# Split parts for four units' gates, a bank of its own for a chain's last product, and other ranks for copies and splits

## The chip, the cores and the metric

The kernel runs on one core of a Trainium2 chip. The metric is the time of one execution in microseconds, as the device takes it; the time before is the median of three timed runs. A separate execution was profiled, and every row of a trace below is from that one.

## The reference

The program is one layer of a decoder trunk over a sequence of 2048 positions with 1024 features, in float32.

```python
h = rms_norm(x, norm1_g)
z = h @ w_in                                   # 1024 -> 3584
lru_x, lru_gate, sc_b, sc_c, sc_x = split(z)   # 1024, 1024, 512, 512, 512
lru_x = causal_dwconv(lru_x, lru_conv_w) + lru_conv_b          # 4 taps
r = sigmoid(lru_x @ wa + ba); i = sigmoid(lru_x @ wx + bx)     # 16 heads of 64
a = exp(-8 r softplus(-lam)); b = sqrt(1 - a^2) * (i * lru_x)
y_lru = scan(h = a h + b) * gelu(lru_gate)
y_sc = sc_b * causal_dwconv(sc_c * sc_x, sc_conv_w)            # 3 taps
x = x + concat(y_lru, y_sc) @ w_out
h = rms_norm(x, norm2_g)
gate, up = split(causal_dwconv(h @ w_up, ffn_conv_w))          # 1024 -> 6144
x = x + (gelu(gate) * up) @ w_down
return rms_norm(x, final_g)
```

## The kernel before, in words

Features lie on the 128 partitions and positions along the free dimension. The sequence is worked on in two halves of 1024 positions (T); a matmul covers a block of 512 (NB). The order of the stages is: in-projection and out-projection of the first half (0 to 332 and 332 to 449 us of the span), the same of the second half (449 to 743 and 743 to 862), then up- and down-projection of the first half (to 1322 and 1551) and of the second (to 2008 and the end).

**Split products.** A float32 product is made of three products in TensorE's one-pass float32 format (fp32r): each operand is split into a high part (a copy on ACT that rounds, L239) and a low part (a subtraction on DVE, L240), and the products hi·hi, hi·lo and lo·hi are added in PSUM (`product_step`, L291, matmuls at L295). The weights of every output block are loaded by SP into a page "wr" and split into "wh" and "wl". One small product was not split: the gates.

**The first half's in-projection** (`in_phase`, L491) begins with the eight blocks of x. Each is loaded, scaled and split into xh and xl (L463, L464), and its products with two (for two blocks three) weight blocks are started at once. Its square (ACT, L309) is added to ss_a (DVE, L310); when all eight are in, the sum is itself split (rh_a, rl_a), multiplied by a matrix of 1/1024 on PE (ms_a, L327), and gives 1/rms, with which every later result is scaled as it leaves PSUM. After that the units follow in the order L0 L1 S0 S1 L2 L3 L4 L5 L6 L7 S2 S3: eight recurrent units (L, 128 channels, two heads of 64 on two halves of the partitions) and four short-convolution units (S). In a recurrent unit PE makes the gate branch's product of this unit and the product of the next one (96 matmuls), then this unit's gates (`lru_gates`, L376, matmuls at L380): for each block of 512 and each half of the partitions one float32 matmul with a 64x128 weight block from "gw", out into four PSUM banks zr and zi. Their moving operand is cv, the unit's convolution (ACT L354, then three DVE steps L356). ACT then takes the sigmoids of the gates (eight of 64x512, L391), and exp, tanh, square and square root in turn (L396 to L400), DVE the scan, and the product with the gelu of the gate branch (L407) is y.

**What is written off.** Results y and combinations of them (yc, yd, made by DVE at L562 to L569) are stored by POOL to the DRAM buffers y_d some steps later (`defer`, `tick`, L236). POOL also adds weight blocks to each other in DRAM by accumulating transfers (so_d, L418). Small temporary tiles (squares, rh, rl, yc, yd, gw) share a pool "tmp" of seven pages of 128x1024: a new tile there waits for the last reader of the page it gets, a store included.

**The second half's in-projection** (`in_blocks`, L907; class `InPair`, L854) multiplies pairs of output blocks by Strassen's scheme with seven products over four 512-wide operands: W11, W12, W22, S1 to S4. A product is 12 matmuls (four K steps, three split products, L689), and three banks serve it: x collects W11, S2, S3 and W22 one after the other, and after each of them ACT copies the running sum out (`copy`, L700), so that the next product in the bank has to wait for the copy; a holds W12; c holds S1 and S4. DVE adds the banks to the copies (`add`, L704). Each turn of the loop works on one pair (`cur`) and finishes the one before it (`prev`): W11 and W12 of cur, W22 of prev, the gates of the last finished recurrent unit, S2 of cur, S4 of prev, and S1 and S3 of cur. In the trace the tiles of the pairs are called xlin, prin, sbin (a pair's first block) and soin (its second), and the banks zxin, zain, zcin.

**What sets the order.** PE, SP and POOL run in the order in which the program is written. On DVE and ACT a scheduler orders the instructions by priority: `tc.high_priority(offset=n)` ranks a block of them n steps ahead of its place in the program. The copies and additions of the pairs, the sigmoids and the results that leave PSUM all have HP = 120; weight splits of the first half have HW = 90; the splits of the second in-projection, the squares and the convolutions of the first half have none.

## Time and profile before

| | us |
|---|---|
| median of three timed runs | 2259.07 (2258.54 to 2259.25) |
| the profiled execution | 2254.52 |
| its span | 2252.5 |
| PE busy in the span | 2223.2 (99%) |
| DVE busy | 1780.7 (79%) |
| ACT busy | 1216.2 (54%) |
| POOL busy | 175.7 (8%) |
| first half's in-projection: 34 to 332 of the span | PE busy 298.0 of 298 |
| second half's, with the first part of its out-projection: 449 to 780 | PE busy 318.9, DVE 240.3, ACT 243.0 of 331 |

PE's granted clock is 0.998 over the span. An engine's row in a timeline begins with the start and the duration in microseconds, then the engine, the source line, the operation, the tiles out<-in and their shape; in square brackets stands how long the engine was idle before the instruction and what ended the wait. A matmul's own duration overlaps the next one's, so the distance of two starts tells its cost. In a table of waits the three numbers are the sum, how often, and the longest.

### The profile page before, as it was taken

The page shows a single profiled execution, that of the slowest core. Times are in us where ns is not written, and L with a number is a line of the kernel's source. Part 1 is how long each engine was busy: PE and PEld are TensorE (multiplying, and loading weights), DVE is VectorE, ACT ScalarE, POOL GpSimd, SP SyncE. Part 2 cuts the span into 40 slices and gives each one's busy share as a digit, 9 for nine tenths or more (in the row PEclk, how much of TensorE's full clock was granted, in tenths as well). Part 3 has the DMA queues.
Part 4 walks back from the last instruction along what each step waited for, and adds up shares of the span by engine and source line. Part 5 has one row for each costly group of instructions (what it writes and reads, how often), then busy time and mean ns, then how long its engine had stood idle before and what let it go on. Part 6 is the DMA issues. An engine that isn't in the chain of part 4 may idle for free.

```text
span 2252.5 us, 26402 instructions
## 1 busy us (share of the span) xinstructions
PE 2223.2 (99%) x9754; PEld 1815.1 (81%) x9754; DVE 1780.7 (79%) x2062; ACT 1216.2 (54%) x1411; POOL 175.7 (8%) x302
## 2 busy tenths in 40 slices
PE   9999999999999899999999999999999999999997
PEld 7887788887767688888888788888888888888886
DVE  8767879847778899898887887676988888886556
ACT  7538835557797554555544454444544444453343
POOL 0021110000000000110111100000000000000000
PEclk9999999999999999999999999999999999999999
DMA  8486369734434874565557477674223232359754
GB/s 313 104 236 187 121 227 303 273 108 136 164 121 128 311 267 169 180 195 173 166 164 222 128 254 243 232 254 137 99 100 111 98 113 90 108 196 346 243 193 156
DMA packets 157953, 415.01 MB, mean 184 GB/s; under 512 B 16640, under 2 KB 19328, under 8 KB 157248
## 3 DMA queue, kind: packets, MB, share of 16 engines
q1 hardware_dynamic: 135872, 354.86, 45.5%
q0 software_dynamic: 21808, 58.47, 10.1%
q8 instruction: 76, 1.25, 0.2%
q14 instruction: 53, 0.43, 0.1%
q10 hardware_dynamic: 144, 0.00, 0.0%
HBM read 311.55 MB, written 139.46 MB: 200 GB/s over the span
## 4 chain that ended last, share of the span: by engine, by line
PE 85%; issue 5%; ACT 4%; DVE 3%; DMA 2%; POOL 0%; SPq 0%; DVEq 0%; ACTq 0%; POOLq 0%
PE zx L689 21%; PE zin_b L295 13%; PE dx L1022 12%; PE zc L689 11%; PE dy L1022 9%; PE ox L1022 5%; PE za L689 5%; PE oy L1022 4%; PE zxin L689 2%; PE zS L689 1%; PE zcin L689 1%; PE zr_b L380 1%; PE zW L689 1%; PE zain L689 1%; ACT wS_in L239 0%
## 5 line engine op out<-in xcount | busy, mean ns | idle before, releaser
L239 ACT ACTIVATE fh_d<-wrf_d 128x1024 fp32r<-128x1024 f32 x84 | 89.0, 1060 | 204.3 <-PE dy L1022 78.4
L240 DVE TENSOR_TENSOR fl_d<-wrf_d,fh_d 128x1024 fp32r<-128x1024 f32 x84 | 102.7, 1223 | 120.7 <-ACT fh_d L239 118.4
L1022 PE MATMUL dx<-fh_d,wl_d 128*128 128x512 f32 x384 | 149.4, 389 | 0.0
L1022 PE MATMUL dx<-fh_d,wh_d 128*128 128x512 f32 x384 | 149.4, 389 | 0.0
L1022 PE MATMUL dx<-fl_d,wh_d 128*128 128x512 f32 x384 | 149.4, 389 | 0.0
L295 PE MATMUL zin_b<-xh,wh_in 128*128 128x512 f32 x448 | 139.4, 392 | 0.2
L295 PE MATMUL zin_b<-xl,wh_in 128*128 128x512 f32 x448 | 138.2, 389 | 0.1
L295 PE MATMUL zin_b<-xh,wl_in 128*128 128x512 f32 x448 | 137.9, 389 | 0.0
L240 DVE TENSOR_TENSOR wla_up<-wra_up,wha_up 128x1024 fp32r<-128x1024 f32 x48 | 58.8, 1224 | 98.3 <-ACT wha_up L239 98.3
L356 DVE SCALAR_TENSOR_TENSOR cg<-ug,prm,cg 128x1024 f32<-128x1024 f32 x96 | 122.8, 1279 | 8.1 <-ACT cg L352 7.3
L356 DVE SCALAR_TENSOR_TENSOR cu<-un,prm,cu 128x1024 f32<-128x1024 f32 x96 | 122.7, 1278 | 4.7 <-ACT cu L352 4.3
L689 PE MATMUL zc<-hhB,whd_up 128*128 128x512 f32 x368 | 120.8, 389 | 0.0
L689 PE MATMUL zx<-ht,whc_up 128*128 128x512 f32 x368 | 113.4, 389 | 0.0
L1022 PE MATMUL dy<-fh_d,wh_d 128*128 128x512 f32 x288 | 112.0, 389 | 0.0
L1022 PE MATMUL dy<-fl_d,wh_d 128*128 128x512 f32 x288 | 112.0, 389 | 0.0
L1022 PE MATMUL dy<-fh_d,wl_d 128*128 128x512 f32 x288 | 112.0, 389 | 0.0
L240 DVE TENSOR_TENSOR wl_d<-wrw_d,wh_d 128x1024 fp32r<-128x1024 f32 x84 | 102.3, 1218 | 8.3 <-ACT wh_d L239 7.0
L700 ACT ACTIVATE ug<-zx 128x512 f32<-128x512 f32 x92 | 54.8, 596 | 98.1 <-PE zx L689 93.1
L295 PEld LDWEIGHTS zin_b<-xh,wh_in 128*128 128x128 f32 x448 | 83.5, 188 | 23.7 <-issue 3.8
L295 PEld LDWEIGHTS zin_b<-xl,wh_in 128*128 128x128 f32 x448 | 84.1, 188 | 18.1 <-DVE xl L464 0.6
L295 PEld LDWEIGHTS zin_b<-xh,wl_in 128*128 128x128 f32 x448 | 84.1, 188 | 17.4
L239 ACT ACTIVATE wh_d<-wrw_d 128x1024 fp32r<-128x1024 f32 x84 | 87.8, 1046 | 11.6 <-PE zc L689 4.0
(552 smaller groups left out, 6332.2 us busy)
## 6 DMA issues: line engine op xcount, KB each, us to landing
wrc_up<-in_w_up SPq DMA_DIRECT2D x48, 512.0 KB, 4.9
f_d_T<-cg SPq DMA_DIRECT2D x96, 256.0 KB, 2.5
wrw_d<-sd_d_S SPq DMA_DIRECT2D x48, 512.0 KB, 4.6
wrf_d<-f_d_T SPq DMA_DIRECT2D x48, 512.0 KB, 4.2
f_d_B<-cu SPq DMA_DIRECT2D x72, 256.0 KB, 2.4
wrw_d<-in_w_down SPq DMA_DIRECT2D x36, 512.0 KB, 4.8
wrf_d<-f_d_B SPq DMA_DIRECT2D x36, 512.0 KB, 3.3
wr_in<-in_w_in SPq DMA_DIRECT2D x25, 512.0 KB, 5.9
```

Source lines behind the costliest of these rows:

```text
L239: nc.scalar.activation(r32(hi), src, AF.Copy)
L240: nc.vector.tensor_tensor(r32(lo), src, hi, ALU.subtract)
L295: nc.tensor.matmul(ps[t], r32(a), r32(b[:, blk(t)]), start=(first and i == 0), stop=(last and i == 2))
L356: nc.vector.scalar_tensor_tensor(dst, src[:, k : k + T], col(o_w + k), dst, ALU.mult, ALU.add)
L380: nc.tensor.matmul(ps[t], gw[rows, :], cv[rows, blk(t)], start=True, stop=True)
L689: nc.tensor.matmul(ps, r32(p[:, s]), r32(self.hs[k][x][o]), start=f and i == 0, stop=l and i == 2, skip_group_check=True,)
L700: nc.scalar.activation(dst, self.x, AF.Copy)
L1022: nc.tensor.matmul(ps[m], r32(p), r32(x[:, k, :]), start=first and i == 0 and n == 0, stop=(last or not on_x) and i == ni - 1 and n == 2, ...
```

## The change

**1. Gates.** For the first half's units L2 to L5 the gates' float32 matmuls (four per unit in the program) become twelve fp32r matmuls from split parts: hi·hi, hi·lo and lo·hi. The four units' gate weights are split once into one page "gp" of the pool "tmp" (ACT and DVE, 128x512 each), and each unit's cv is split into ch and cl (ACT and DVE, 128x1024 each, rank 60).

**2. The start.** The squares and their additions get rank 20.

**3. The second in-projection.** W22's product gets a bank of its own, and DVE adds it to the running sum that S3 left (`part`, `sum`); ACT's copy of it falls away, and S3 is the last product in bank x. W11's and S3's copies go to the other half of the pair's tiles, from where the sums are made. The copies' rank goes from 120 to 200 (in the up-projection too, which shares `copy`), and the splits of the weights get rank 100.

**4.** MK = 0 leaves the order of PE's product steps at the start as it was.

```diff
+MK = 0
+XP = 200
+AP = 120
+QP = 20
+IWQ = 100
+APART = ("W22",)
+LAST_X = "S3"
+GQ = 60
+PARTS = (2, 3, 4, 5)
...
+    def lru_gates_of_parts(c, half, cv, gw):
+        pss = [pst2(f"z{name}{half}_{c}") for name in "ri"]
+        hi, lo = (flat(act(f"c{x}{half}_{c}")) for x in "hl")
+        with tc.high_priority(offset=GQ):
+            split(hi, lo, cv)
+        for i, (a, b) in enumerate(((gw[0], hi), (gw[0], lo), (gw[1], hi))):
+            for t in range(T // NB):
+                for ps, rows in zip(pss, HALVES):
+                    nc.tensor.matmul(ps[t], r32(a[rows, :]), r32(b[rows, blk(t)]), start=i == 0, stop=i == 2)
+        return pss
+
+    gate_parts = []
+
+    def gates_of(c, half, cv):
+        if c not in PARTS:
+            return lru_gates(c, half, cv, gate_w[0][:, c, :])
+        if not gate_parts:
+            n = max(PARTS) + 1 - min(PARTS)
+            t = flat(tmp("gp"))
+            for i in range(2):
+                gate_parts.append(t[:, i * n * P // 1 : (i + 1) * n * P].rearrange("p (c k) -> p c k", c=n))
+            split(*gate_parts, gate_w[0][:, min(PARTS) : max(PARTS) + 1, :])
+        return lru_gates_of_parts(c, half, cv, [g[:, c - min(PARTS), :] for g in gate_parts])
...
         for k in range(KC):
-            x_square(half, k, acc, xs[k])
+            with tc.high_priority(offset=QP):
+                x_square(half, k, acc, xs[k])
...
+        ps_2 = pss[2]
+        for k in range(2, 2 + MK):
+            product_step(ps_2, wcol(wts[2], k), acts[k], False, k == KC - 1)
         parts = mean_split(acc, f"a{half}")
...
-        ps_2 = pss[2]
-        for k in range(2, KC):
+        for k in range(2 + MK, KC):
             product_step(ps_2, wcol(wts[2], k), acts[k], False, k == KC - 1)
...
-                gates = lru_gates(c, half, cv, gate_w[0][:, c, :])
+                gates = gates_of(c, half, cv)
...
         def copy(self, dst):
-            with tc.high_priority(offset=HP):
+            with tc.high_priority(offset=XP):
                 nc.scalar.activation(dst, self.x, AF.Copy)
 
         def add(self, dst, ps):
-            with tc.high_priority(offset=HP):
+            with tc.high_priority(offset=AP):
                 nc.vector.tensor_tensor(dst, ps, dst, ALU.add)
...
             t = home(f"w{op}_in{i}")
-            split(t[:, 0, :], t[:, 1, :], raw[:, at, :])
+            with tc.high_priority(offset=IWQ):
+                split(t[:, 0, :], t[:, 1, :], raw[:, at, :])
...
+        def part(self, w, x, dst, src):
+            if w in APART:
+                ps = pst(f"z{w}{self.name}")
+                self.run(ps, w, x, True, True)
+                self.sum(dst, ps, src)
+            else:
+                self.run(self.x, w, x, False, w == LAST_X)
+                self.copy(dst)
+
+        def sum(self, dst, ps, src):
+            with tc.high_priority(offset=AP):
+                nc.vector.tensor_tensor(dst, ps, src, ALU.add)
+
         def first_term(self):
-            self.begin()
+            self.open()
+            self.x = pst(f"zx{self.name}")
+            self.run(self.x, "W11", "B11", True, LAST_X == "W11")
+            self.copy(self.g[1])
 
         def second_term(self):
-            self.second()
+            a = pst(f"za{self.name}")
+            self.run(a, "W12", "B21", True, True)
+            self.sum(self.g[0], a, self.g[1])
 
         def third_term(self):
             self.sum1()
 
         def fourth_term(self):
-            self.run(self.x, "S2", "T2", False, False)
-            self.copy(self.g[1])
+            self.part("S2", "T2", self.g[1], self.g[1])
 
         def fifth_term(self):
-            self.run(self.x, "S3", "T3", False, False)
             self.open_second()
-            self.copy(self.n[1])
-            self.add(self.n[1], self.c)
+            self.part("S3", "T3", self.n[0], self.g[1])
+            self.sum(self.n[1], self.c, self.n[0])
 
         def sixth_term(self):
             self.end()
 
         def seventh_term(self):
-            self.fourth()
+            self.part("W22", "T4", self.n[0], self.n[0])
+            self.second_done()
```

In the changed file line numbers are 9 higher from `split` on, and more further down. Where the scheduler put things shows in the order of instructions on ACT and DVE. At the start, on ACT, from the sixth block of x on (xh is the high part, sq the square, rh_a the high part of their sum); before:

```order
L463 ACTIVATE xh0_6_458<-x0_6_457,g1_71 128x1024
L309 ACTIVATE sq_a0_6_509<-x0_6_457 128x1024
L463 ACTIVATE xh0_7_476<-x0_7_475,g1_71 128x1024
L239 ACTIVATE wh_in0_1_316<-wr_0_2_290 128x256 x3
L309 ACTIVATE sq_a0_7_512<-x0_7_475 128x1024
L239 ACTIVATE rh_a0_526<-ss_a0_287 128x1024
```

and with the change:

```order
L496 ACTIVATE xh0_6_458<-x0_6_457,g1_71 128x1024
L318 ACTIVATE sq_a0_6_509<-x0_6_457 128x1024
L318 ACTIVATE sq_a0_7_512<-x0_7_475 128x1024
L248 ACTIVATE wh_in0_1_316<-wr_0_2_290 128x256 x3
L496 ACTIVATE xh0_7_476<-x0_7_475,g1_71 128x1024
L248 ACTIVATE rh_a0_526<-ss_a0_287 128x1024
```

The last square has moved ahead of the third weight block's three pieces and of the last xh. DVE, whose additions and subtractions follow, has moved in the same way: its last addition to ss_a now stands ahead of the three wl pieces and of the last xl, and the four sums of weights behind them.

In the first half, ahead of the gates of L2, on ACT (sv0_1 is the second short-convolution unit's result; xs4 is a block of the second half's x, squared beside; cv0_2 the convolution that L2's gates read); before:

```order
L352 ACTIVATE sv0_1_1189<-pr0_1_1114,prm_73 128x1024
L1097 ACTIVATE xs4_1622<-xs4_1622 128x1024
L239 ACTIVATE wh_in0_12_1627<-wr_in0_12_1626 128x1024
L354 ACTIVATE cv0_2_1259<-xl0_2_1254,prm_73 128x1024
L239 ACTIVATE wh_in0_5_1695<-wr_in0_5_1694 128x1024
L1097 ACTIVATE xs5_1792<-xs5_1792 128x1024
```

and with the change:

```order
L361 ACTIVATE sv0_1_1189<-pr0_1_1114,prm_73 128x1024
L248 ACTIVATE gp_1402<-gw_524 128x512
L1151 ACTIVATE xs4_1649<-xs4_1649 128x1024
L248 ACTIVATE wh_in0_12_1654<-wr_in0_12_1653 128x1024
L363 ACTIVATE cv0_2_1259<-xl0_2_1254,prm_73 128x1024
L248 ACTIVATE wh_in0_5_1722<-wr_in0_5_1721 128x1024
L248 ACTIVATE ch0_2_1409<-cv0_2_1259 128x1024
L440 ACT_TABLE_LOAD
```

The copy of the gate weights' high part stands between sv0_1 and xs4, and the copy of cv0_2 behind the weights' split. On DVE, at the same place, before:

```order
L567 TENSOR_TENSOR yd0_3_1264<-sv0_1_1189,sv0_0_978 128x512
L568 SCALAR_TENSOR_TENSOR yc0_2_1041<-yc0_2_1041,sv0_1_1189 128x512
L569 SCALAR_TENSOR_TENSOR yd0_3_1264<-yc0_2_1041,sv0_1_1189 128x512
L1098 TENSOR_TENSOR ss_a1_744<-ss_a1_744,xs4_1622 128x1024
L340 MEMSET xl0_5_1756 128x3
```

and with the change:

```order
L603 TENSOR_TENSOR yd0_3_1264<-sv0_1_1189,sv0_0_978 128x512
L604 SCALAR_TENSOR_TENSOR yc0_2_1041<-yc0_2_1041,sv0_1_1189 128x512
L249 TENSOR_TENSOR gp_1402<-gw_524,gp_1402 128x512
L605 SCALAR_TENSOR_TENSOR yd0_3_1264<-yc0_2_1041,sv0_1_1189 128x512
L1152 TENSOR_TENSOR ss_a1_744<-ss_a1_744,xs4_1649 128x1024
L349 MEMSET xl0_5_1795 128x3
```

The subtraction for the low part stands between yc0_2 and the second half of yd0_3. Tile gp has the page that yc0_0 had; that tile's readers are the POOL stores to T1 and T2 of the first pair of units.

In the second in-projection, on ACT, around the sigmoids of unit L3 (r1_3, i1_3); soin7 and xlin8 are the pairs' tiles that are copied from bank x; before:

```order
L700 ACTIVATE soin7_4813<-zxin7_4716 128x512
L239 ACTIVATE wW12_in9_4832<-wr_in9W12_8W22_4829 128x512
L391 ACT_TABLE_LOAD
L391 ACTIVATE r1_3_4907<-zr1_3_b0_4899,prm_73 64x512
L391 ACTIVATE i1_3_4908<-zr1_3_b0_4899,prm_73 64x512
L391 ACTIVATE r1_3_4907<-zr1_3_b1_4900,prm_73 64x512
L391 ACTIVATE i1_3_4908<-zr1_3_b1_4900,prm_73 64x512
L391 ACTIVATE r1_3_4907<-zi1_3_b0_4901,prm_73 64x512
L391 ACTIVATE i1_3_4908<-zi1_3_b0_4901,prm_73 64x512
L391 ACTIVATE r1_3_4907<-zi1_3_b1_4902,prm_73 64x512
L391 ACTIVATE i1_3_4908<-zi1_3_b1_4902,prm_73 64x512
L700 ACTIVATE xlin8_4856<-zxin8_4858 128x512
```

and with the change:

```order
L440 ACTIVATE soin7_4858<-soin7_4858 128x1024
L424 ACT_TABLE_LOAD
L424 ACTIVATE r1_3_4965<-zr1_3_b0_4957,prm_73 64x512
L424 ACTIVATE i1_3_4966<-zr1_3_b0_4957,prm_73 64x512
L424 ACTIVATE r1_3_4965<-zr1_3_b1_4958,prm_73 64x512
L424 ACTIVATE i1_3_4966<-zr1_3_b1_4958,prm_73 64x512
L424 ACTIVATE r1_3_4965<-zi1_3_b0_4959,prm_73 64x512
L424 ACTIVATE i1_3_4966<-zi1_3_b0_4959,prm_73 64x512
L736 ACTIVATE xlin8_4913<-zxin8_4915 128x512
L248 ACTIVATE wW22_in8_4892<-wr_in9W12_8W22_4886 128x512
L424 ACTIVATE r1_3_4965<-zi1_3_b1_4960,prm_73 64x512
L424 ACTIVATE i1_3_4966<-zi1_3_b1_4960,prm_73 64x512
```

The copy of soin7 has gone, its gelu has moved from behind the scan's exp to a place ahead of the sigmoids, and xlin8's copy stands behind six of them instead of all eight.

## The prediction

> **What bounds the kernel now.** I read the page's busy times first, then the table of stages, then PE's waits. The change touches the start, the first half's in-projection and the second half's; of the last two, in microseconds: the stretch, its length, and the busy time (with instructions) of PE, its weight loads, DVE, ACT and POOL.
>
> ```profile
> 34.00:332.00 298.00, 298.00 (x1304) 237.42 (x1304) 231.26 (x304) 180.99 (x189) 46.64 (x76) 1.00 0.57 178
> 449.00:780.00 331.00, 318.94 (x1382) 250.89 (x1380) 240.31 (x288) 242.97 (x316) 22.99 (x43) 1.00 0.47 159
> ```
>
> In the first half (34 to 332) PE never idles: only fewer or shorter matmuls can shorten it, and any wait that the change brings is a loss in full. In the second stretch (449 to 780: the second in-projection and the head of its out-projection) PE idles 12.1 us. The table of PE's waits says on what (total, times, longest; what is not in these rows lies in the out-projection, where weights have to be loaded first, or outside this stretch):
>
> ```profile
> PE zxin L689 <- ACT soin L700: 2.3, 3, 0.8
> PE zcin L689 <- DVE soin L704: 1.9, 1, 1.9
> PE zxin L689 <- ACT sbin L700: 1.5, 1, 1.5
> PE zxin L689 <- ACT xlin L700: 1.4, 2, 1.0
> PE ms_a L327 <- ACT rh_a L239: 1.1, 1, 1.1
> PE ms_a L327 <- DVE rl_a L240: 0.5, 1, 0.5
> ```
>
> The change can reach the zxin rows (PE wants to go on in a bank that ACT still has to copy) and the two ms_a rows (the start).
>
> **The start.** ACT, DVE and PE, in order of time:
>
> ```profile
> 23.15 1.14 ACT L463 ACTIVATE xh<-x,g 128x1024 fp32r<-128x1024 f32 x1
> 24.19 1.01 ACT L239 ACTIVATE wh_in<-wr 128x256 fp32r<-128x256 f32 x3
> 25.11 1.05 ACT L309 ACTIVATE sq_a<-x 128x1024 f32<-128x1024 f32 x1
> 26.14 1.28 DVE L464 SCALAR_TENSOR_TENSOR xl<-x,g,xh 128x1024 fp32r<-128x1024 f32 x1
> 27.34 0.75 DVE L240 TENSOR_TENSOR wl_in<-wr,wh_in 128x256 fp32r<-128x256 f32 x2
> 30.15 1.22 DVE L310 TENSOR_TENSOR ss_a<-ss_a,sq_a 128x1024 f32<-128x1024 f32 x1
> 28.52 0.62 PE L295 MATMUL zin_b<-xh,wh_in 128*128 128x512 f32 x2
> 30.79 0.61 PE L295 MATMUL zin_b<-xh,wl_in 128*128 128x512 f32 x2
> 32.51 0.73 PE L327 MATMUL ms_a<-rh_a,ones_r 128*128 128x512 f32 x2 [1.10 <-ACT rh_a L239]
> 33.77 0.73 PE L327 MATMUL ms_a<-rl_a,ones_r 128*128 128x512 f32 x2 [0.53 <-DVE rl_a L240]
> ```
>
> A pair of full matmuls takes 0.455 us here (28.52 to 30.79 is five of them). From 30.79 to 32.51 and from 32.51 to 33.77 PE steps 1.72 and 1.26 us, so 1.27 + 0.81 = 2.1 us are lost; that is 0.4 to 0.5 more than the two idle times, and I take 0.25 us for a restart below. With the squares ranked up, the last square takes the ACT place at 23.15, the three weight pieces end at about 25.1, and the last xh at 26.2. On DVE the last addition then starts at 26.14, the three subtractions of weights (two take 0.75) end at 28.5, and the last xl at 29.7. The mean's matmuls find everything ready, but PE wants that xl as its second pair of the last step, at 28.98: it waits 0.8, with the restart 1.0. Gain 2.1 - 1.0 = **1.1 us** (0 if ACT gets the last x too late to square it first, 2.1 if nothing waits).
>
> **The gates.** All four products of a unit, now in fp32:
>
> ```profile
> 155.71 0.69 PE L380 MATMUL zr_b<-cv,gw 64*128 64x512 f32 x1
> 155.71 0.69 PE L380 MATMUL zi_b<-cv,gw 64*128 64x512 f32 x1
> 156.24 0.59 PE L380 MATMUL zr_b<-cv,gw 64*128 64x512 f32 x1
> 157.10 0.59 PE L380 MATMUL zi_b<-cv,gw 64*128 64x512 f32 x1
> 157.62 0.73 PE L295 MATMUL zin_b<-xh,wh_in 128*128 128x512 f32 x2
> ```
>
> The two row halves start together, four times, 0.43 us apart; from 155.71 to 157.62 the unit costs 1.91 us, of which 1.7 are the four and 0.2 the edges. The new form has six pairs of a single-pass product. The nearest row for one is the full matmul, 0.455 / 2 = 0.227 us, so 6 x 0.227 = 1.36, and with the edges 1.56: 0.35 saved, four times **-1.4 us**. The other bound: halves that run one after the other, 12 x 0.227 + 0.2 = 2.92, which is 4 x 1.0 = +4.0 us. I take the first, since the fp32 pairs overlap here in full. [...]
>
> **What the parts wait for.** The gate weights' parts take one page of the small pool (seven pages), and by the order of instructions that page is the one that held yc of the first pair. ACT's copy stands after the second sv, DVE's subtraction between yc and the last yd. Both now wait for the two POOL stores that read this page:
>
> ```profile
> 129.35 0.76 POOL L236 DMA_DIRECT2D y_d_T<-yc  x1
> 136.32 0.96 POOL L418 DMA_DIRECT2D so_d_S<-so_d_S  x1 [6.21 <-issue]
> 136.92 0.96 POOL L236 DMA_DIRECT2D y_d_T<-yc  x1
> DMA to landing us min/median/max: 9.7/9.7/9.7
> ...
> DMA to landing us min/median/max: 7.7/7.7/7.7
> 134.76 0.69 DVE L568 SCALAR_TENSOR_TENSOR yc<-yc,sv 128x512 f32<-128x512 f32 x1
> 139.59 1.22 DVE L1098 TENSOR_TENSOR ss_a<-ss_a,xs 128x1024 f32<-128x1024 f32 x1 [3.43 <-ACT xs L1097]
> 150.58 1.22 DVE L240 TENSOR_TENSOR wl_in<-wr_in,wh_in 128x1024 fp32r<-128x1024 f32 x1
> 157.46 1.22 DVE L1098 TENSOR_TENSOR ss_a<-ss_a,xs 128x1024 f32<-128x1024 f32 x1 [5.66 <-ACT xs L1097]
> ```
>
> The landing rows are those of the two stores: the one issued at 136.92 ends at 146.6, the one issued at 129.35 at 137.1. POOL's issues are held up by the accumulating transfers ahead of them (6.21 us before 136.32), not by PE, so a faster start does not move them. Behind ACT's copy stand the square of xs, two weight splits and cv of the third recurrent unit; behind DVE's subtraction stands all that DVE did from 139.59 to 151.8, which is 12.2 us without a gap. Started at about 146.6 + 0.7 + 0.6 (the subtraction and the yd), that ends at 160.1, and the new subtraction of cv's parts (1.2) at **161.3**. PE reaches these gates at 155.71 before, or 1.1 earlier with the faster start: it now waits until about 161.3, so 6.7 us are lost against 154.6. DVE's gap of 5.66 us before 157.46 absorbs most of what is late; for the next unit I get its parts within 1 us of PE's arrival, and take 0 (0 to 1.5). Bounds of the stall: 4 us, if the store lands earlier by the start's gain and more; 8 with the next unit; and nothing at all if it has landed by 141, which is rival A.
>
> **The second in-projection.** ACT is what is full there:
>
> ```profile
> 612.00:635.00 23.00, 21.24 (x92) 16.23 (x92) 14.52 (x19) 22.35 (x29) 0.00 (x0) 1.00 0.34 109
> 635.00:659.00 24.00, 21.74 (x94) 16.22 (x92) 19.59 (x23) 23.72 (x31) 2.69 (x5) 1.00 0.42 142
> 615.29 0.68 ACT L391 ACTIVATE r<-zr_b,prm 64x512 f32<-64x512 f32 x1
> 620.89 0.60 ACT L700 ACTIVATE xlin<-zxin 128x512 f32<-128x512 f32 x1
> 629.14 1.06 ACT L407 ACTIVATE soin<-soin 128x1024 f32<-128x1024 f32 x1
> 630.74 3.01 PE L689 MATMUL zxin<-htx,wW_in 128*128 128x512 f32 x12 [0.74 <-ACT soin L700]
> 645.57 0.50 PE L689 MATMUL zxin<-hhB11x,wS_in 128*128 128x512 f32 x1 [1.52 <-ACT sbin L700]
> 654.76 3.03 PE L689 MATMUL zxin<-htx,wW_in 128*128 128x512 f32 x12 [0.74 <-ACT soin L700]
> ```
>
> The copies stand behind eight sigmoids (615.29 to 620.89, 0.70 each). Four edits answer to PE's waits:
> - W22 in its own bank waits for no copy. The two waits at 630.74 and 654.76 (0.74 each) go with their restarts: -2.0. The third soin wait gains nothing: at 739.85, next in the pair's order, PE waits 1.9 us for DVE's soin anyway (the zcin row).
> - xlin's copy (1.0 in the waits) now stands behind six sigmoids, and no soin copy ahead of it (0.5), but the unit's gelu (629.14, 1.06) has moved ahead: 1.4 + 0.5 - 1.0 = 0.9 earlier, and the wait is nearly gone: -1.1 with its restart.
> - sbin's copy (1.52) stands behind three sigmoids, so 3.5 earlier, but then the product in its bank is the last to come: I take 1.2 of 1.8.
> - The small xlin wait of the next cycle goes: -0.3.
>
> Sum **-4.6**. The thirteen W22 sums go to DVE, whose 240.31 busy of 331 leave room for 13 x 0.69 (the yc row's length) = 9.0; ACT loses thirteen copies of about 0.6 and two table loads. Bounds: -2.0 if ACT's fullness only moves the copies' waits, -6 if the waits for prin and the first xlin went as well.
>
> **Sum.** -1.1 + 6.7 - 1.4 - 4.6 = -0.4. The profiled execution took 2254.52 us (2.02 outside its span of 2252.5), so its counterpart would take 2254.1; the median of the timed runs lies 4.55 higher, which nothing here changes: 2254.1 + 4.55, so **2258.6**. Changes of under 0.2% (4.5 us) can't be told from none.
>
> **Rivals.**
> - A, no stall: the stores land by 141, or the planner's page is free by then. For it: the store issued at 129.35 has landed by 137.1, and only one of the two is late. Against: the second is issued at 136.92, behind an accumulation. -1.1 - 1.4 - 4.6 = -7.1, so 2252.0. Chance 0.28.
> - B, a longer stall, the case on the slower side. The place is the same store. One more wait of POOL like the 6.21 us before 136.32 puts the landing at 152.8, and everything behind the two waiting instructions is that much later: -0.4 + 6.2 = +5.8, so 2264.9. It decides for slower from a landing at about 151.5. For it: the store shares its queue with transfers that take 9.7 us; against: POOL's order is as before. Chance 0.13.
> - C, the gates' halves don't overlap in the new form: +4.0 in place of -1.4, +5.0 in all, so 2264.1 with the stall. For it: single-pass products are new to this shape. Against: two halves share nothing in the rows above, where both start at 155.71. Chance 0.08.
> - D, ACT stays the bound of the second in-projection and its waits return at the gates and scans, with 2.0 recovered: +2.2, so 2261.3. For it: 22.35 of 23 and 23.72 of 24 us. Against: ACT has some slack over the whole stage (242.97 of 331). Chance 0.09.
>
> **How the numbers follow.** My forecast has 0.42; its own range, from 4 to 8 us of stall and 2 to 6 recovered, is 2254.5 to 2262.5. Faster by over 0.2%: nearly all of A and a little of the forecast, 0.31. Slower: B, half of C, and a little of the rest, 0.20. Within: 0.49. The range reaches down to A with 1.5 us below it and up to B: 2250.5 to 2265.
>
> **What would show it.** At the third recurrent unit's gates PE waits for cl (or ch) some 6 us, ACT's copy of gp ends near 147 and DVE idles before its subtraction: forecast; with no such idle time, A. The gates' pairs step 0.23 us (0.45: C). The ms_a waits are gone and one zin_b waits about 0.8 for xl. No zxin wait on soin is left, the sbin and xlin waits sum to under 1 us, and ACT's table loads are 72; if PE's idle time in that stage stays over 10 us, D. A gain of over 8 us, or a stall at the later units' gates too, would prove the sum wrong.

## The result, and the profile after

The changed kernel takes 2267.22 us (median of six runs, 2263.97 to 2269.83) against 2258.91 for the kernel before (six runs, 2256.41 to 2259.25): 1.0038 times, with an interval of 1.0025 to 1.0051. It is slower by 8.3 us, and the time lies above the predicted range. Its profiled execution took 2267.84 us, of which 2265.9 are span.

Where PE waits now (profile after, PE's waits: microseconds in total, times, longest):

```profile
PE zr_b L400 <- DVE cl L249: 5.4, 4, 1.9
PE zx L725 <- ACT ug L736: 3.4, 2, 2.3
PE zxin L725 <- ACT xlin L736: 3.3, 2, 2.2
PE zr_b L400 <- ACT ch L248: 2.8, 3, 1.1
PE zcin L725 <- DVE soin L920: 2.6, 1, 2.6
PE zr_b L389 <- DVE cv L365: 1.8, 2, 1.3
PE zxin L725 <- ACT prin L736: 1.3, 1, 1.3
PE zin_b L304 <- DVE xl L497: 0.9, 1, 0.9
```

The two ms_a waits of the start are gone and one wait for xl has come, as forecast. No wait for soin's copy on ACT is left in the second in-projection, but xlin, prin and DVE's soin cost more than before, and PE waits for cv ahead of the second half's gates (the L389 row), where it did not wait before. New are the waits for the gates' parts, ch and cl: 8.2 us in all, at four units and not at one. A row by stage, before and then after (stretch, length, busy time of PE, its weight loads, DVE, ACT and POOL; then the granted clock, the share of the DMA engines and GB/s):

```profile
34.00:341.80 307.80, 307.80 (x1347) 245.54 (x1347) 240.88 (x315) 187.05 (x195) 46.64 (x76) 1.00 0.58 182
```

```profile
34.00:341.80 307.80, 299.63 (x1314) 239.48 (x1314) 234.88 (x309) 182.77 (x193) 46.71 (x77) 0.99 0.55 172
```

PE, which before never idled in this stretch, now idles 8.2 us there. The loss can be dated by the start of each unit's gates on PE (in the first half L0, L2 to L6, and the first matmul of the mean over the second half's x, with which the stage ends):

| first half, us | L0 | L2 | L3 | L4 | L5 | L6 | end |
|---|---|---|---|---|---|---|---|
| before | 53.51 | 155.71 | 179.61 | 203.51 | 227.41 | 251.31 | 331.65 |
| after | 52.04 | 155.24 | 181.19 | 207.54 | 233.81 | 261.17 | 341.52 |
| after - before | -1.46 | -0.47 | 1.58 | 4.03 | 6.41 | 9.86 | 9.86 |

The start gains 1.46, and from L0 to L6 11.3 us are lost: 0.99 up to L2's gates, then 2.05, 2.45, 2.38 and 3.46 from one unit's to the next.

**L2, where I forecast the one stall.** POOL, ACT and DVE, and how long the store issued at 134.37 took to land:

```profile
134.37 0.96 POOL L245 DMA_DIRECT2D y_d_T<-yc  x1
DMA to landing us min/median/max: 7.4/7.4/7.4
141.89 0.63 ACT L248 ACTIVATE gp<-gw 128x512 fp32r<-128x512 f32 x1 [13.12 <-DMA y_d_T<-yc]
142.55 0.69 DVE L249 TENSOR_TENSOR gp<-gw,gp 128x512 fp32r<-128x512 f32 x1 [8.46 <-ACT gp L248]
163.76 1.06 ACT L1151 ACTIVATE xs<-xs 128x1024 f32<-128x1024 f32 x1 [6.20 <-DMA xs<-in_xT]
164.85 1.23 DVE L1152 TENSOR_TENSOR ss_a<-ss_a,xs 128x1024 f32<-128x1024 f32 x1 [7.75 <-ACT xs L1151]
```

The wait for the store is there, and on both engines: 13.12 us on ACT. It ended at 141.9, not at 146.6, so L2's gates were held up less than I said (behind it DVE ran from 143.16 to cl at 155.88 without a gap, as I had counted):

```profile
155.24 0.49 PE L400 MATMUL zr_b<-ch,gp 64*128 64x512 f32 x1 [0.92 <-ACT ch L248]
157.15 0.50 PE L400 MATMUL zr_b<-cl,gp 64*128 64x512 f32 x1 [1.18 <-DVE cl L249]
157.49 0.39 PE L400 MATMUL zr_b<-cl,gp 64*128 64x512 f32 x1
157.72 0.39 PE L400 MATMUL zr_b<-ch,gp 64*128 64x512 f32 x1
158.28 0.74 PE L304 MATMUL zin_b<-xh,wh_in 128*128 128x512 f32 x2
```

The pairs step 0.23 us (157.49 to 157.72): the halves overlap in full, and without the two waits a unit's gates are about as short as I worked out. (In the trace a float32 product is two rows on PE, eight for a unit's four, whose pairs are 0.43 us apart from the second on; an fp32r product is one, twelve for twelve.) But the gap on DVE that was to absorb the delay is itself a wait, for a load of xs that in the kernel after is later too: its square on ACT stands at 163.76 against 156.37 before, and DVE's gap grew from 5.66 to 7.75 us. The load comes later because SP issues it later (before, then after):

```profile
149.53 0.33 SPq L1102 DMA_DIRECT2D xs<-in_xT  x1
153.69 0.33 SPq L1156 DMA_DIRECT2D xs<-in_xT  x1
```

Both issues follow the end of L2's convolution on DVE by 0.06 us (149.47 and 153.63), and that convolution stands behind the subtraction for gp. So what holds DVE up ahead of the gap moves the gap's end as well. The rest of the 7.4 us is the load's own duration, 6.7 us before and 10.0 after. In seven of the traces below the square, which waits for the load, starts 8.6 to 10.3 us after that convolution's end (6.9 before, 10.1 after), and the 10.3 are of the one with no part made by then, so nothing says that this rest comes from the change.

**The units after it.** ACT and DVE run a loop, once per unit: sigmoids, exp and the rest, the scan, the next unit's xl, its convolution, the next sigmoids. The rows of one turn, ACT and DVE in the order of time, after:

```profile
170.00 0.68 ACT L424 ACTIVATE r<-zr_b,prm 64x512 f32<-64x512 f32 x1
180.10 1.04 ACT L248 ACTIVATE ch<-cv 128x1024 fp32r<-128x1024 f32 x1
181.59 1.23 DVE L249 TENSOR_TENSOR cl<-cv,ch 128x1024 fp32r<-128x1024 f32 x1
183.40 1.06 ACT L440 ACTIVATE g<-g 128x1024 f32<-128x1024 f32 x1
185.76 1.06 ACT L433 ACTIVATE cv<-cv 128x1024 f32<-128x1024 f32 x1
194.70 1.25 ACT L363 ACTIVATE cv<-xl,prm 128x1024 f32<-128x1024 f32 x1 [5.98 <-DVE xl L464]
197.26 0.69 ACT L424 ACTIVATE r<-zr_b,prm 64x512 f32<-64x512 f32 x1
```

and the rows of the kernel before that answer to the sigmoids, the square root, the gelu, the convolution and the next sigmoids:

```profile
163.62 0.68 ACT L391 ACTIVATE r<-zr_b,prm 64x512 f32<-64x512 f32 x1
176.10 1.06 ACT L400 ACTIVATE cv<-cv 128x1024 f32<-128x1024 f32 x1
178.48 1.06 ACT L407 ACTIVATE g<-g 128x1024 f32<-128x1024 f32 x1
185.32 1.25 ACT L354 ACTIVATE cv<-xl,prm 128x1024 f32<-128x1024 f32 x1 [3.89 <-DVE xl L431]
187.88 0.68 ACT L391 ACTIVATE r<-zr_b,prm 64x512 f32<-64x512 f32 x1
```

Before, a turn takes 187.88 - 163.62 = 24.3 us; after, 197.26 - 170.00 = 27.3, and PE's own period is 23.9 (203.51 - 179.61). The next three turns take 25.6, 23.2 and 24.6 us before and 26.4, 24.2 and 26.1 after. The copy ch stands inside the loop, ahead of the square root; the gelu, with its table load, has slipped ahead of the square root too (183.40 ahead of 185.76, where it was 178.48 behind 176.10). Of the 3.0 us by which this turn grew, ch is 1.0, and the gelu with its table load (182.10 to 184.47) is most of the rest. The square root comes 15.8 us after the first sigmoid instead of 12.5, and the scan, xl and the next sigmoids come later with it. The loop began 6.4 us late (170.00 for 163.62; in the traces below in which no parts are made by then it begins between 162.1 and 167.0), and it is slower than PE.

### The profile page after: what moved, and what is told of

The parts are those of the page before. It is cut to its first block, busy times and chain, and to the rows that moved or that the text cites. A ratio compares the mean times of both kernels' runs of the same rounds, so it can differ in the third digit from the quotient of the medians.

```text
span 2265.9 us, 26455 instructions
## 1 busy us (share of the span) xinstructions
PE 2226.8 (98%) x9770; PEld 1820.3 (80%) x9770; DVE 1793.2 (79%) x2080; ACT 1212.1 (53%) x1401; POOL 176.7 (8%) x302
## 4 chain that ended last, share of the span: by engine, by line
PE 74%; issue 8%; DVE 7%; ACT 5%; DMA 4%; POOL 1%; SPq 1%; DVEq 0%; POOLq 0%; ACTq 0%
PE zx L725 20%; PE dx L1076 12%; PE zc L725 10%; PE dy L1076 9%; PE zin_b L304 5%; PE za L725 5%; PE ox L1076 3%; PE zxin L725 3%; PE oy L1076 2%; PE zcin L725 1%; PE zS L725 1%; PE zain L725 1%; PE zW22in L725 1%; DMA wrc_up<-in_w_up 1%; PE zW L725 1%
```

## The experiments

The question was which part of the gates' change loses the time, the late store or the longer loop, and why the second in-projection gave nothing back. All kernels are the changed one with the edit shown, unless it says otherwise; ratios are to the kernel before on the same chip, with their intervals. 0.001 is 2.26 us.

### The rest of the change without the gates

The gates' parts left out; the start, the own bank and the ranks stay:

```diff
-PARTS = (2, 3, 4, 5)
+PARTS = ()
```

> The changed kernel with no unit's gates from parts (start and second in-projection stay changed). If the gates are what makes the change slower (the profile has PE 11.3 us later over the gates of L2 to L5), this comes out within 2 us of before, 2257 to 2261, and the in-projection of the first half ends about 1.5 us earlier than before. If the second in-projection is as much to blame (3.1 us later in the profile), it stays 2 to 4 us above before, 2261 to 2263.

Measured: 2256.95, 0.9994 (0.9984 to 1.0003). So the gates cost 1.0038 - 0.9994 = 0.0044, or 9.9 us, and all else together gives 1.4 us, which can't be told from nothing; I had put it at 5.7. The gates of the first half start 1.69 us earlier throughout. That is the start, so the second in-projection gains nothing that these times can tell.

The start alone (the kernel before, with the squares' rank):

```diff
-            x_square(half, k, acc, xs[k])
+            with tc.high_priority(offset=20):
+                x_square(half, k, acc, xs[k])
```

> The kernel before with the squares' rank of 20 alone. The runs with the new start had L0's gates 1.6 to 2.2 us earlier (53.5 before), and PE never idles from there to the end of the first in-projection: 1.6 to 2.2 us below before, about 2256 to 2257. If what comes early at the start is waited for again at the next place that a transfer sets, the time is that of before.

Measured: 2257.84, 0.9991 (0.9982 to 1.0). This is as much as the kernel with the start and the second in-projection's edits together. In its trace the gates of L0 to L6 start 1.60 us earlier than before, but the matmul at which PE waits for DVE's soin, late in the second in-projection, starts at 740.00, against 739.85: there the gain is gone. So it is not shown that the 2.0 us of the ratio are those of the start.

The ranks without the own bank:

```diff
-APART = ("W22",)
-LAST_X = "S3"
+APART = ()
+LAST_X = "W22"
-PARTS = (2, 3, 4, 5)
+PARTS = ()
```

> Gates as before; W22 back in bank x with ACT's copy; the new ranks and the new start kept. If the W22 bank is what put the wait into ACT's queue (gelu of soin ahead of the sigmoids, waiting for DVE's sum), the xlin wait at about 621 falls from 2.2 to 1.0 us or less and the second in-projection gets shorter: 1 to 3 us below the kernel with the gates as before, 2254 to 2256. If the ranks are to blame, it stays at 2257 to 2259.

Measured: 2255.87, 0.9989 (0.9979 to 0.9999): the lowest ratio of all, and the only one whose interval lies below 1. PE's waits for soin on ACT are back (5.0 us in five), the xlin and prin waits are small (0.3 each).

The own bank without the ranks:

```diff
-XP = 200
+XP = 120
-IWQ = 100
+IWQ = 0
-PARTS = (2, 3, 4, 5)
+PARTS = ()
```

> Gates as before; W22 in its own bank; the ranks of copies and splits as they were; the new start kept. The W22 waits (0.74 us, twice) are gone. If the ranks are to blame for the xlin and ug waits that grew (xlin 2.2, ug 2.6 us in the up-projection), both fall to 1.0 and 1.4: 1 to 3 us below the kernel with the gates as before, 2254 to 2256; if the bank is, 2257 to 2259.

Measured: 2259.67, 1.0006 (0.9996 to 1.0015), though the start is in it. The two largest of PE's waits are these:

```profile
PE zxin L725 <- DVE wW_in L249: 2.7, 2, 2.1
PE zxin L725 <- ACT sbin L736: 2.4, 1, 2.4
```

The own bank moves PE's wait from soin to the weights' parts and sbin. What it does with the ranks is seen in the first kernel of this section, around the sigmoids whose rows the prediction shows at 615.29 and 620.89 (ACT, and PE's matmul that waits for the copy):

```profile
614.40 1.06 ACT L440 ACTIVATE soin<-soin 128x1024 f32<-128x1024 f32 x1 [1.84 <-DVE soin L920]
616.76 0.68 ACT L424 ACTIVATE r<-zr_b,prm 64x512 f32<-64x512 f32 x1
620.96 0.60 ACT L736 ACTIVATE xlin<-zxin 128x512 f32<-128x512 f32 x1
621.61 0.50 PE L725 MATMUL zxin<-hhB11x,wS_in 128*128 128x512 f32 x1 [2.22 <-ACT xlin L736]
```

soin's gelu now waits 1.84 us for W22's sum on DVE, ahead of the sigmoids on ACT. The first sigmoid starts at 616.76 (615.29 before), and the xlin copy, two sigmoids earlier in the order, still at 620.96 (620.89 before). PE arrives earlier and waits 2.2 for it, where it waited 1.0, and in the four microseconds that follow (622 to 626) its granted clock is 0.57 (from 622.18 on two matmuls take 0.82 us; from 616.96 on two took 0.61). PE's wait for cv ahead of the second half's gates, new in the profile after, goes with the own bank: 1.3 and 1.4 us in the two runs with it, 0.3 with the ranks alone, none with the start alone.

The ranks alone, with the copies of the up-projection at their old rank:

```diff
-            with tc.high_priority(offset=XP):
+            with tc.high_priority(offset=XP if self.name.startswith("in") else HP):
```

(with the edit for "the ranks without the own bank")

> Gates as before, W22 in bank x with ACT's copy, new start, new ranks in the second in-projection; the copies of the up-projection at their old rank of 120. If the copies' rank of 200 is what made the ug waits of the up-projection longer (2.8 us against 1.4), they fall back and the time is about 1 us below the same kernel with the new rank there, 2254 to 2256; if not, 2255 to 2257.

Measured: 2258.29, 0.9991 (0.9982 to 1.0), no different from the ranks alone. PE's waits for ug sum to 2.3 us here, 2.8 there and 2.7 with the start alone, so that the changed kernel waits 3.4 for ug, where the profile before has 1.4, cannot be put down to this rank.

### Making the parts, without using them

All parts are made, and PE takes the old float32 gates from cv and gw:

```diff
-        for i, (a, b) in enumerate(((gw[0], hi), (gw[0], lo), (gw[1], hi))):
-            for t in range(T // NB):
-                for ps, rows in zip(pss, HALVES):
-                    nc.tensor.matmul(ps[t], r32(a[rows, :]), r32(b[rows, blk(t)]), start=i == 0, stop=i == 2)
+        for t in range(T // NB):
+            for ps, rows in zip(pss, HALVES):
+                nc.tensor.matmul(ps[t], gate_w[0][rows, c, :], cv[rows, blk(t)], start=True, stop=True)
```

> The changed kernel makes all parts (gp, ch, cl) but PE takes the gates in fp32 from cv and gw as before, so PE doesn't wait for parts. Theory L: the sigmoids of L2, L3, L4, L5 still start 26 to 27 us apart (as in the changed kernel: 170.0, 197.3, 223.7) although PE runs at 23.9 per unit, since ACT and DVE set the pace; PE waits nowhere at the gates; the time is that of the kernel with the gates as before, 2256 to 2259. If the distance were set by PE's waits (the rival), the sigmoids come 24 to 25.6 us apart as before the change.

Measured: 2265.19, 1.0032 (1.0018 to 1.0046). So nearly all that the gates cost (0.0038 of 0.0044, or 8.6 of 9.9 us) comes with making the parts, and PE loses it although it waits for none of them:

```profile
PE zr_b L399 <- DVE cv L365: 3.8, 1, 3.8
PE zin_b L304 <- DVE g L463: 3.3, 4, 1.8
```

The first row is L2's gates: in this execution the store landed late, gp started on ACT at 146.17, 4.3 us later than in the profile after, and L2's convolution came later with it. The profiled execution is the slowest of the six (2269.87), so its trace shows more than the median loses. The second row is the bound on PE's lead: it wants the next product's bank and DVE has not yet read g out of it. Theory L was wrong on the time, which was to be 2256 to 2259. The sigmoids of L2 to L5 start 25.3, 26.6 and 24.4 us apart, of which only the second lies in its 26 to 27; with the gates as before they are 24.3, 25.6 and 23.3. A turn is longer by ch's 1.0 to 1.1 us and no more. In this run and in the one with cv's parts alone ch stands behind the square root and nothing has slipped ahead of that (ACT, cv's parts alone):

```profile
176.23 1.06 ACT L429 ACTIVATE cv<-cv 128x1024 f32<-128x1024 f32 x1
177.19 1.05 ACT L248 ACTIVATE ch<-cv 128x1024 fp32r<-128x1024 f32 x1
```

From the start of the gates to the first sigmoid of that unit I read, for the five units L2 to L6 (us):

| kernel | L2 | L3 | L4 | L5 | L6 |
|---|---|---|---|---|---|
| before | 7.9 | 8.3 | 10.0 | 9.3 | 10.0 |
| gates as before | 9.5 | 9.9 | 11.6 | 11.0 | 11.6 |
| cv's parts made, unused | 9.6 | 11.0 | 13.7 | 14.2 | 14.5 |
| gate weights' parts made, unused | 15.3 | 15.7 | 15.4 | 14.3 | 13.3 |
| all parts made, unused | 15.7 | 15.4 | 17.4 | 16.0 | 14.5 |
| after | 14.8 | 16.1 | 16.2 | 14.1 | 12.8 |

With the gate weights' or cv's parts made PE gets 14 to 17 us ahead of the sigmoids, and where the parts are not used it then waits for the next product's bank (PE's zin_b on DVE's g: 3.3 us with all parts made, 2.8 with the gate weights', 0.2 with cv's). In the kernel before, by the table, about 6 us of that are free. The bound belongs to this order of the instructions: with the parts ahead of the sigmoids (below) PE is up to 25 us ahead.

The gate weights' parts alone (the float32 matmuls of the last edit; ch and cl left out, gp made and not used):

```diff
-        hi, lo = (flat(act(f"c{x}{half}_{c}")) for x in "hl")
-        with tc.high_priority(offset=GQ):
-            split(hi, lo, cv)
```

> The changed kernel with the gate weights' parts made (and not used), no ch and cl, gates in fp32 from cv and gw. Theory S (the page of the small pool, and with it ACT and DVE held until the store lands): about 4 us lost at L2's gates, as in the run in which all parts were made and not used (3.9), and the later units lose nothing: 2259 to 2262. Theory L (the copies and subtractions of cv in each unit's loop): L2 loses at most 2, and the time is within 2 us of the kernel with the gates as before, 2256 to 2259.

Measured: 2261.79, 1.0013 (1.0004 to 1.0022), that is +4.3 us on the kernel with the gates as before. gp waits 13.68 us for the store here too, and the first sigmoid of L2 stands at 169.2 instead of 163.6. L2 and L3 are in time on PE (both -1.86 against before); L4 loses 2.04 and L6 1.69. The time is in Theory S's range, but not for its reason: L2 was to lose about 4 us and the later units nothing, and it is the other way round. (This trace is of the fastest of the ten runs, 2258.81.)

The parts of cv alone (the same matmuls; gp left out, ch and cl made and not used):

```diff
-            t = flat(tmp("gp"))
...
-            split(*gate_parts, gate_w[0][:, min(PARTS) : max(PARTS) + 1, :])
+            gate_parts.extend([gate_w[0][:, min(PARTS) : max(PARTS) + 1, :]] * 2)
```

> The changed kernel with ch and cl made for L2 to L5 (and not used), no parts of the gate weights, gates in fp32. Theory S: no engine waits for a y_d store, nothing is late, 2256 to 2259. Theory L: each unit from L3 on loses 1 to 2 us at PE's wait for a bank that DVE has not read (zin_b for g, 3.3 us over four waits in the run with all parts), the sigmoids start 25 to 26.5 us apart, 2260 to 2264.

Measured: 2258.55, 0.9998 (0.9988 to 1.0007): +0.9 us, which can't be told from nothing. The sigmoids of L2 to L5 start at 163.72, 189.02, 215.65 and 240.05; with the gates as before at 163.6, 187.8, 213.4 and 236.7. They fall behind by 1.1 us with every unit, which is the length of ch on ACT, and on PE nothing is lost up to L5; from there to the end of the stage 1.7 us are. So the distances are Theory L's and the time is Theory S's.

My reading is that the two halves of the cost do not simply add: the store uses up the 6 us of PE's free lead at once, the copies use 1.1 of it per unit, and once the lead is gone, what is late on ACT and DVE is lost on PE. The times alone do not show this: 4.3 and 0.9 us against the 8.6 of both leave a difference of 3.4, and by the intervals of the four ratios that is uncertain by about 5. The traces show its parts, the late first sigmoid in one run and the longer turns in the other.

### Attempts to mend it

Gate weights' parts made at the start, long before the stores (the block that splits gw moved behind the decay rates):

```diff
         decay_rates(dz)
+        split_gates()
```

> The changed kernel with the gate weights split at the start, into the page of a square that is long free: no wait for stores, ACT and DVE not held before L2. Theory S: ch and cl come in time at L2 and L3, and what follows is in time too, 2257 to 2260. Theory Q: L2 is in time (1 to 2 us recovered) and a part of L3, but L4 and L5 still wait 1.3 and 3 us, 2263 to 2266.

Measured: 2267.04, 1.0044 (1.0029 to 1.0059), as slow as the change itself. The wait has a new owner (DVE):

```profile
143.41 0.69 DVE L605 TENSOR_TENSOR yd<-sv,sv 128x512 f32<-128x512 f32 x1 [9.55 <-DMA y_d_T<-yc]
```

What both theories start from, that no engine waits for a store, did not hold: now yd waits for the page that the stores still read. The pool of seven is a page short at this place, whichever tile comes last.

The parts of cv made right behind the convolution, ahead of the sigmoids (a call in the loop over the units; the tiles are kept for the gates):

```diff
                 if nxt[0] == "L":
                     cur = (lru_conv(nxt[1], half, ps_n, rs),)
+                    if nxt[1] in PARTS:
+                        cv_parts[nxt[1]] = parts_of(nxt[1], half, cur[0])
```

> The changed kernel with each cv split right behind its convolution, so that the copy ch stands ahead of the previous unit's sigmoids on ACT and takes another page; the gate weights' page still waits for the stores. Theory Q (ch stands in ACT's queue behind eight sigmoids, exp and tanh of the unit before, in every unit): the waits for ch and cl at L3, L4 and L5 go, 6 to 8 us are recovered, 2259 to 2261. Theory S (the wait for the stores makes everything behind it late, and L3 to L5 only inherit it): L3 to L5 stay late, within 2 us of the changed kernel, 2265 to 2268.

Measured: 2272.45, 1.0064 (1.0047 to 1.008): slower than both theories allow, and worse than the change itself by 0.0026, or 5.9 us. ch reaches the head of ACT's queue before DVE has finished the convolution, and the sigmoids, whose input is ready (the first starts at 205.77 with no wait of its own, right behind its table load), stand behind it:

```profile
203.40 1.06 ACT L248 ACTIVATE ch<-cv 128x1024 fp32r<-128x1024 f32 x1 [7.44 <-DVE cv L365]
```

Both of these together (with GQ at 130):

> Both of the two edits before this one: parts ahead of the sigmoids, gate weights split at the start. Both theories: no wait at the gates of L2 to L5, and each unit's six pairs cost 1.6 us in place of 1.9: the first in-projection ends 1.5 (start) + 1.4 (gates) = 2.9 us earlier than before. Total then 1 to 2 us below the kernel with the gates as before.

Measured: 2271.91, 1.0065 (1.005 to 1.008), where both theories had it faster than before, with yd waiting 11.67 us and ch 4.0 and 7.4.

gp from the pool of 28 large pages instead of the seven:

```diff
-            t = flat(tmp("gp"))
+            t = flat(act("gp"))
```

> The changed kernel with the gate weights' parts in a page of the pool of 28 instead of the pool of seven, so that neither they nor the next yd have to wait for the stores of yc. Theory S (one page of the small pool is missing, and whoever comes next waits for a store; L3 to L5 inherit its 6 to 7 us): no engine idles for y_d stores before L2, L2 to L5 in time, 2256 to 2259. Theory L (a unit's loop over ACT and DVE, from its sigmoids over the scan to the next convolution, takes 26 to 27 us with the copy and the subtraction in it, longer than PE's 23.9, and the gates are now tied to it): L2 and L3 in time, 3 to 5 us recovered, but L4 and L5 late by 1 to 3 us each, 2261 to 2264.

Measured: 2272.74, 1.0057 (1.0035 to 1.0079). This run left no trace that can be set beside the others, so the same kernel was run once more:

> The same kernel as in the run with the gate weights' parts in the pool of 28 pages, for a trace that can be compared. Theory P (pages are short in both pools: whatever new tile comes takes the place of one whose store is not through): ACT no longer waits for a y_d store before L2, but DVE or ACT wait for si_d stores ahead of ch and cl of L3 to L5, and the distance from gates to sigmoids is 12 to 16 us by L4. Theory L alone: no wait for si_d stores; distance 9.5 at L2 and growing by 1.5 to 2.5 per unit to 14 or more at L4, with PE's waits only from there.

Measured: 2268.94, 1.0045 (1.0029 to 1.006). No instruction waits for a y_d store any more, and L2 and L3 are in time; then L4 loses 4.27 and L5 6.07 us, and cl waits for another store, 2.71 us at L3, 3.33 at L4 and 3.79 at L5 (DVE, L3):

```profile
179.34 1.23 DVE L249 TENSOR_TENSOR cl<-cv,ch 128x1024 fp32r<-128x1024 f32 x1 [2.71 <-DMA si_d<-sb]
```

ch and cl take pages of that pool in which weight sums (sa, sb) wait to be written off. Taking away the one wait that I had predicted thus gains nothing: in the large pool it is taken over by the stores of the sums.

Only one unit from parts:

```diff
-PARTS = (2, 3, 4, 5)
+PARTS = (5,)
```

> The changed kernel with parts for L5 alone. The distance from gates to sigmoids is still 9.5 to 11.6 us up to L4, so L5's parts come in time; the six pairs save 0.35 us, and nothing else is left of the first half's change: within 1 us of the kernel with the gates as before, 2256 to 2259, unless gp, which by the order waits for the stores of a yd, holds ACT there as it did before L2: then 2 us or more above it.

Measured: 2267.31, 1.0032 (1.0021 to 1.0044): one unit costs nearly as much as four. L2 to L4 are in time; at L5 both parts of the gate weights are made late, behind ch and a gelu on ACT, and PE waits for each:

```profile
233.91 0.79 PE L400 MATMUL zr_b<-ch,gp 64*128 64x512 f32 x1 [7.70 <-ACT gp L248]
237.52 0.79 PE L400 MATMUL zr_b<-ch,gp 64*128 64x512 f32 x1 [1.54 <-DVE gp L249]
```

Around this stall PE ran at half clock (the stretch, its length, PE's busy time and so on):

```profile
229.86:243.51 13.65, 8.07 (x23) 5.47 (x24) 13.37 (x15) 9.63 (x12) 0.00 (x0) 0.50 0.03 12
```

Half of the 8.07 busy microseconds, 4.0, are lost to that. With the two waits (9.2) and less the 0.35 that one unit saves it makes up the 12.9 us that this trace loses from L0 to L6.

In this execution a load of xs was late as well (its square on ACT at 160.12, after 9.69 us of waiting), so that the first sigmoid of L2 stood at 166.96 with no part made yet; how much of the 7.70 us is due to that is not separated. What the rows do show is that the parts are made when PE needs them, not when an engine is free. A kernel that makes them early, with pages of their own and off the loop, was not run; whether it can keep the 0.35 us per unit stays open.

## Why the prediction was wrong

By the ratios, the parts of the change are worth, beside what I forecast: the start -2.0 us (-1.1 forecast), the second in-projection +0.7 (0.9994 less 0.9991; -4.6 forecast), the gates +9.9 (6.7 - 1.4 = +5.3 forecast). Of the 9.0 us between the two sums, the second in-projection is 5.3, the gates are 4.6, and the start takes back 0.9. The intervals leave the start uncertain by about 2 us, the second in-projection by 3 and the gates by 3.5.

**The start** was right in kind: the waits for the mean are gone, the wait for xl is 0.93 us (0.8 forecast), and the gates of L0 come 1.46 earlier in the trace (1.1 forecast).

**The stall at L2: right place, wrong size.** gp does wait for the store, 13.12 us. But the landing at 146.6 was a sum of an issue time and a duration from one execution. In the changed kernel POOL issued the store 2.55 us earlier (134.37), and it took 7.4 instead of 9.7. That a faster start does not move POOL's issues was wrong: with the start alone the same store is issued at 135.02, for 136.92 before. POOL's next issue does follow the landing of the transfer into so_d ahead of it, by about 0.3 us in both: issued at 128.06 before, that transfer landed 8.0 us later and the next issue came at 136.32; after, it was issued at 126.71, landed 6.8 us later, and the next issue came at 133.77. PE waited 0.92 + 1.18 us there, not 6.7.

**The step that failed is "DVE's gap of 5.66 us before 157.46 absorbs most of what is late; for the next unit I get its parts within 1 us of PE's arrival, and take 0 (0 to 1.5)".** From L2's gates to those of L6 the units lost 2.05, 2.45, 2.38 and 3.46 us, which is the sign that the prediction itself names as proof against its sum, a stall at the later units' gates too. Two things were wrong in it. The gap was a wait for a load, and the load came later too, because SP issues it when L2's convolution on DVE ends (0.06 us behind it in both profiles). And I costed ch and cl as if they lay beside the other work, without asking how long a turn of ACT's and DVE's loop takes: 24.3 us against PE's 23.9 (24.4 over the four turns from L2 to L6), so there was nothing to catch up with. A delay of 6 us then stays for the rest of the units, and each unit's parts add to it. The trace of before had this in two rows (163.62 and 187.88). I left them unread because PE did not wait there.

The 11.3 us lost from L0 to L6 are made up so: waits for ch and cl 8.2, less 1.4 for four shorter gates (4 x 0.35), plus 3.4 for two stretches of half clock, which I had not in the sum at all, and 1.1 left for seven restarts, 0.16 each:

```profile
183.00:187.00 4.00, 4.00 (x14) 2.77 (x15) 1.10 (x2) 3.96 (x5) 0.16 (x1) 0.57 1.06 272
187.00:192.00 5.00, 5.00 (x23) 4.13 (x22) 4.94 (x6) 1.72 (x2) 0.78 (x1) 1.00 0.71 112
237.00:241.00 4.00, 4.00 (x14) 2.91 (x13) 2.09 (x3) 3.97 (x5) 0.00 (x0) 0.58 0.33 132
```

In four microseconds after the stalls of L3 and L5 the granted clock is 0.57 and 0.58, so 4 x 0.43 and 4 x 0.42 us are lost, and PE is at full clock again in the next stretch. The 1.1 is what is left over, not measured by itself.

**A second step failed: the second in-projection's -4.6.** By the ratios it is the larger share of the error, and no gain came; one of 2 us can't be told from none by them. The waits that I meant to remove went, and others came in their place. With the gates as before, PE's waits for soin's and sbin's copies (2.3 and 1.5 us) are gone; xlin has 1.2 us more, prin 0.9, the weights' parts 1.0, and cv ahead of the gates 1.3. I let the gelu of soin move ahead of the sigmoids at a price of its length (1.0), and did not ask what it waits for: the W22 sum on DVE, 1.84 us away. With ACT's 22.35 busy of 23 us in that stretch there was no room for it. And I put the thirteen sums on DVE at nothing, where PE's wait for DVE's cv came with the own bank. Rival D said this much of ACT (it stays the bound) and still left 2.0 recovered; by its sign, over 10 us of idle time of PE in that stage, it is met (10.9 of 331 us from 458.9 on, 12.1 before). The ranks without the own bank were at least as good.

**The rivals.** C is refuted by the 0.23 us step. A fails at its condition, since the store that gp waits for landed at 141.8 and PE did wait; but the 2.1 us of that wait are nearer to its nothing than to my 6.7. B had the right sign and a time close by (2264.9), but its mechanism, a later landing at L2, is not what the profile after shows; the landing was earlier. That the time lies near was luck. A landing as late as the one before the change does occur: in the run with all parts made and not used gp started at 146.17, and PE waited 3.8 us at L2. The slower case that did happen, a loop on ACT and DVE that is no faster than PE, was not among them, and it should have had a chance of its own.

Last, 4.55 us between the profiled execution and the median were carried over as something "which nothing here changes". The profile before has full clock after its waits (the last section shows the rows); that of the kernel with the start alone has two half-clock stretches, and they cost 2 x 1.7 = 3.4 us. So the profiled execution seems to have been a lucky one, and the difference of the two profiles (13.3 us) overstates the change by 5.0.

## What to carry to other kernels

Where one engine is full, look at the loop that feeds it: the distance from one turn's first instruction to the next's, beside the full engine's period, and how far that engine is ahead. An instruction added to a loop of nearly the same period (24.3 us beside 23.9 here) made each turn longer by its own length, 1.1 us for ch with cv's parts alone, however much idle time its engine shows in the sum; PE loses that once its lead is used up. Before a gap is counted as slack, see what ends it, and whether that comes later as well (DVE's gap of 5.66 us grew to 7.75); and before a tile is given a page, see which store still reads it, since taking that wait away for one tile only handed it to another here (yd 9.55 us, or cl 2.71 to 3.79).

## What the runs showed of the hardware

After some waits of 0.8 to 2.4 us PE's granted clock was 0.57 or 0.58 over 4 us soon behind them, and after others of 0.9 to 2.0 us it stayed at 1.00. The stalls of the changed kernel ahead of 183 and 237 us are of one or two microseconds (0.81 and 0.95 at L3, 1.05 and 1.94 at L5). Those at L2, 0.92 and 1.18 us, are no shorter than L3's, and behind them PE stays at full clock; behind L3's its granted clock is 0.50 for 3.41 us:

```profile
157.50:161.50 4.00, 4.00 (x22) 3.01 (x19) 0.00 (x0) 0.06 (x1) 0.00 (x0) 1.00 0.91 252
183.00:186.41 3.41, 3.41 (x12) 2.29 (x13) 0.95 (x1) 3.37 (x4) 0.00 (x0) 0.50 1.10 264
```

In the second half the kernel before and the one with the start alone, whose edit lies 700 us earlier, wait at the same two places. Before, the stretches after a wait of 1.94 us (ended at 739.85) and one of 1.95 (780.49):

```profile
739.80:744.00 4.20, 4.15 (x18) 3.46 (x19) 0.00 (x0) 4.10 (x6) 0.00 (x0) 1.00 1.03 408
780.50:784.50 4.00, 4.00 (x18) 3.31 (x19) 4.00 (x5) 2.33 (x3) 0.00 (x0) 1.00 0.93 339
```

With the start alone, after a wait of 2.43 us (740.00) and one of 1.79 (780.51):

```profile
741.00:745.00 4.00, 4.00 (x12) 3.11 (x11) 0.50 (x1) 3.90 (x6) 0.00 (x0) 0.57 1.03 401
782.00:786.00 4.00, 4.00 (x12) 3.16 (x11) 4.00 (x5) 1.54 (x2) 0.00 (x0) 0.57 0.86 297
```

The same matmuls, the same waits within half a microsecond: full clock in one, 0.57 over 4 us in the other, a loss of 1.7 us each time. So a stall of 0.8 to 2.4 us cost another 1.7 us in some places here and nothing in others, and one trace does not tell which is usual. No run here shows what decides between the two.

POOL's store of yc into y_d took 9.7 us from issue to landing before and 7.4 after. ACT's gp, which waits for that transfer, started at 141.89 us in the changed kernel (store issued at 134.37) and at 146.17 in the kernel that makes the parts and does not use them (issued at 135.96).
